# Portions of GDN's solve inside projections, and the residual's scale and bias behind y

## The chip, the cores and the metric

The kernel runs on one core of one Trainium2 chip. The metric is the device time of one execution in microseconds (us). Each version is run several times; the median counts.

## The reference, cut to what matters

A decoder trunk of four layers over 512 tokens of width 1024, in float32. Each layer has a token mixer (Gated DeltaNet, HGRN2, GLA, Gated DeltaNet) and a SwiGLU channel mixer; both add to the scaled residual and are followed by a layer norm.

```python
for i in range(DEPTH):
    m = mixer_i(x)                        # GDN, HGRN2, GLA, GDN
    x = layer_norm(DN_ALPHA * x + m, mix_ln_g[i], mix_ln_b[i])
    x = layer_norm(DN_ALPHA * x + swiglu(x, ffn_w_in[i], ffn_w_down[i]), ffn_ln_g[i], ffn_ln_b[i])

def gated_deltanet(...):                  # per chunk of 64 tokens
    L = strict_lower(einsum('bhncd,bhnsd->bhncs', k * beta, k) * decay)
    sol = triangular_solve(L + eye(CHUNK), [v * beta, k * beta * exp(G)])
    ...
    o = gated_rms_norm(o, z, norm_w)      # o * rsqrt(mean(o*o)) * norm_w * silu(z)
    return o @ w_out
```

## The kernel before

Tokens stand in NT = 4 row tiles of 128, the width in KD = 8 tiles of 128. A float32 product is made of three matmuls on TensorE (PE) of operands split in a high and a low part (`mm3`, lines 183, 184 and 185). Weights stream from DRAM on SyncE's queue; ScalarE (ACT) casts the high part (`whi`, L144) and VectorE (DVE) subtracts for the low part (`wlo`, L147). PSUM is two pools of four banks: `acc` holds projections (`pj`), `mx` the rest. A tile scheduler sets the order of each engine from the order in which the program is written and from its priorities; inside `manual_schedule` PE keeps the written order. `behind(ins)` holds operations on DVE behind the instruction `ins`.

**GDN's solve.** `gdn` takes the eight heads in two batches, in layers 0 and 3, so there are four solves. `values()` makes eight projections of a batch (v, v, z, z, v, v, z, z; each 24 matmuls of 128x512), and `solve` the inverse of the triangular matrices of 16 chunk blocks. It begins with a chain on DVE that ends in `td` and `ud` (two transposes, L849). Then come four stages of small matmuls on PE: the first (L859) and the second (L865) 64 of 16x16, the third (L877) and the fourth (L891) two bursts of 16 of 32x32 each; between two stages ACT or DVE copies the result (`yt`, `td`, `y2`). A trace counts two rows for one float32 matmul, so that 64 show as 128. Two stages of 64x64 (`y3`, L902 and L908) end the solve. `solve` is a generator: `yield 4` or `yield 1` lets as many projections be written ahead of what follows, and the first stage is held behind the last matmul of the fourth of them (`filled`).

**Output projection and norm.** `out_proj` reads the residual `x` (eight half tiles of 128x512, `get_x`) and calls `down_norm`. In layers 1, 2 and 3 what was stored is the normed residual without the scale and bias of the FFN norm, so `work` has to multiply each half tile by `lnp` (L256) and add `lnp` (L257): 16 operations on DVE. Four `lnp` tiles come by DMA into three buffers (tag `tr`). `work` is called once for each k in `down_part` and holds its operations behind `heads_end`, the last scaling `on*occ` of the heads (L533). The last heads are transposed on PE (`ytp`, L543), DVE makes `y` from them (L550), ACT its high part (`xTh`, L468), DVE its low part (`xTl`, L469); the matmuls `dn` of k = 6 and 7 (4 to 7 in layer 3) need these. `down_part` makes the first half of the columns for all row tiles, `add_x` (L352) adds them to x, `bn_stats` follows (L370). Of the second half, the program writes by hand the order on PE: `down(0)`, `down(1)`, three matmuls of `down(2)`, `tr(0)`, the rest of `down(2)`, and so on. `norm(i)` stands behind `down(i)`: `add_x`, `bn_stats`, the aggregate (L385) and nine small steps to L398 on DVE, then ACT norms the two halves of x (L403), and `tr(i)` transposes x on PE (`xtp`, L221).

Of the kernel before, what the change touches and what calls it, by code (L numbers as in the profile page):

```python
# [13 lines left out]
ALU = mybir.AluOpType  # L14
# [23 lines left out]
class Net:  # L38
    def __init__(self, ctx, tc, a, out):
        self.tc, self.nc, self.a, self.out = tc, tc.nc, a, out  # L40
        pool = lambda name, bufs, **kw: ctx.enter_context(tc.tile_pool(name=name, bufs=bufs, **kw))
        self.cp = pool("const", 1)
        self.raw = pool("raw", 2)
        self.wsp = pool("wsplit", 6)
        self.xp = pool("xT", 1)
        self.ar = pool("arena", 1)
        self.col = pool("cols", 2)
        self.mid = pool("mid", 1)
        self.dr = pool("dram", 2, space=bass.MemoryType.DRAM)
        self.acc = pool("acc", 4, space=PSUM)  # L50
        self.mx = pool("mx", 4, space=PSUM)
        self.n = 0
        self.deferred, self.late, self.lmask, self.x_gb = [], [], None, None
        self.norm_end = self.heads_end = None
        self.todo = []
        self.lo_eng = self.nc.vector
        self.xT = tuple(self.xp.tile([P, KD, T], F32R, name=n) for n in ("xTh", "xTl"))
        self.consts()
# [133 lines left out]
    def proj_cols(self, ps, wt, s, m=P):  # L192
        (wh, wl), (xh, xl) = wt, self.xT
        if wl is None:
            for k in range(KD):
                for x in (xl, xh):
                    self.nc.tensor.matmul(ps[:m, s], wh[:, k], x[:, k, s], start=k == 0 and x is xl,
                                          stop=k == KD - 1 and x is xh)
            return
        for k in range(KD):  # L200
            self.mm3(ps[:m, s], (wh[:, k], wl[:, k]), (xh[:, k, s], xl[:, k, s]), k == 0, k == KD - 1)

    def begin(self, wts):

# [134 lines left out]
    def down_part(self, kt, w, k0, dh, pool, alpha):  # L339

        ps = [self.bank(pool, [P, 512], "dn") for _ in range(NT)]
        k1 = k0 + len(kt)
        for k, wt in self.kblocks(w, dh, k0, k1):
            for i in range(NT):
                self.mm_tok(ps[i], i, kt[k - k0], wt, k == k0, k == k1 - 1)
            self.work()
        for i in range(NT):
            self.add_x(ps[i], i, dh, alpha)

# [5 lines left out]
    def down_norm(self, kt, w, k0, pools, alpha, g, b, to_dram, to_out, rtags):  # L355

        nc, V = self.nc, self.nc.vector
        n = len(kt)
# [156 lines left out]
    def finish(self, heads, ss, dv, nw, tag, facs=None):  # L515


        nc, V = self.nc, self.nc.vector
        n = len(heads)
        c = self.small([P, 2, n * NT], s="occ", bufs=2)  # L520
        if facs is not None:
            V.scalar_tensor_tensor(c[:, 0], ss, SCALE * SCALE / dv, facs[1], ALU.mult, ALU.mult)
            V.tensor_scalar(c[:, 0], c[:, 0], RMS_EPS, None, ALU.add)
        else:
            V.tensor_scalar(c[:, 0], ss, SCALE * SCALE / dv, RMS_EPS, ALU.mult, ALU.add)
        self.rsqrt(c[:, 1], c[:, 0], n * NT, "o")
        if facs is not None:
            V.scalar_tensor_tensor(c[:, 1], c[:, 1], SCALE, facs[0], ALU.mult, ALU.mult)
        else:
            V.tensor_scalar(c[:, 1], c[:, 1], SCALE, None, ALU.mult)  # L530
        todo = [(on, k, e) for k, (ons, gates) in enumerate(heads) for e, on in enumerate(ons)]
        for on, k, e in todo:
            op = V.tensor_tensor(on, on, c[:, 1, k * NT:(k + 1) * NT, None].broadcast_to([P, NT, P]), ALU.mult)  # L533
        self.heads_end = op.ins
        self.deferred += [(on, nw[e], heads[k][1][e], tag) for on, k, e in todo]

    def flush(self):

        todo, self.deferred = self.deferred, []
        for n, (on, nw, gate, tag) in enumerate(todo):  # L540
            pt = self.bank(self.mx, [P, T], "ytp")
            for i in range(NT):
                self.nc.tensor.transpose(pt[:, i * P:(i + 1) * P], on[:, i], self.ident)  # L543
            if tag == "yy":
                yy = yy if n % 2 else self.pair()
                y = yy[:, n % 2]
            else:
                y = self.t2(tag, s="y")
            gate = gate[0][gate[1]]
            self.nc.vector.scalar_tensor_tensor(y, pt, nw, gate, ALU.mult, ALU.mult)  # L550
            yield y

    def gdn(self, layer, j):
# [109 lines left out]
        for b in range(H // NB):  # L663
# [91 lines left out]
                        yield  # L755

            fill = values()
            for n in self.solve(ntf, gd):
                for _ in range(n):
                    next(fill, None)  # L760
            for _ in fill:
                pass

# [51 lines left out]
    def solve(self, nt, gd):  # L815
# [4 lines left out]
        hc = nt.shape[1]  # L820
# [26 lines left out]
        td, ud = sv((P, hc, 32), "td"), sv((P, hc, 32), "ud")  # L847
        for dst, src in ((td, U), (ud, U.rearrange("p s c -> p c s"))):
            V.transpose(dst.rearrange("p h (e c) -> p c e h", e=2), src[:, :, None, :].broadcast_to([P, 16, 2, 16]))  # L849
        yield 4  # L850
        filled = self.last_mm

        py = self.bank(self.mx, [P, 2, hc, 16], "iy")
        S.activation(py.rearrange("p a h c -> p (a h c)"), self.ident[:, None, :].broadcast_to([P, 4, P]), AF.Copy, scale=0.0)
        pu = py[:, 1]
        with self.behind(filled):
            for i in range(hc):
                for q, r in enumerate(half):
                    mm(py[r, 0, i], nt[r, i, 32 * q + 16:32 * q + 32], td[r, i, 0:16], start=True, stop=True)  # L859
        yt = sv((P, hc, 16), "yt")  # L860
        S.copy(yt, py[:, 0])
        yield 1
        for i in range(hc):
            for r in half:
                mm(pu[r, i], yt[r, i], ud[r, i, 16:32], start=True, stop=True)  # L865
        V.scalar_tensor_tensor(ud[:, :, 16:32], ud[:, :, 16:32], self.hi16[:, 1:2], pu, ALU.mult, ALU.add)
        V.tensor_scalar(ud[:, :, 0:16], ud[:, :, 0:16], self.hi16[:, 0:1], None, ALU.mult)
        V.transpose(td, ud)
        yield 1

        y2 = sv((P, hc, 32), "y2")
        pu = self.bank(self.mx, [P, hc, 32], "iu")
        py = self.bank(self.mx, [P, hc, 32], "iy")
        for q in (0, 2):
            r1, r2 = quads[q], quads[q + 1]
            for i in range(hc):
                mm(py[r2, i], nt[r1, i, r2], td[r1, i], start=True, stop=True)  # L877
            S.copy(y2[r2], py[r2])
        for r in quads:
            G.tensor_copy(nt[r, :, r], ud[r])  # L880
        hh = hc // 2
# [1 line left out]
        for g in range(2):  # L883
            G.memset(t64[g][0:32, :, 32:64], 0.0)
            for r in quads[:2]:
                S.copy(t64[g][r, :, r], td[r, g * hh:(g + 1) * hh])
        yield 1
        for q in (0, 2):
            r1, r2 = quads[q], quads[q + 1]
            for i in range(hc):  # L890
                mm(pu[r1, i], y2[r2, i], ud[r2, i], start=True, stop=True)  # L891
            if q == 0:
                for g in range(2):
                    V.transpose(t64[g][32:64, :, 0:32], pu[r1, g * hh:(g + 1) * hh])
            V.tensor_copy(nt[r1, :, r2], pu[r1])
        yield 1
        lo, up = slice(0, 64), slice(64, P)
        for g in range(2):
            y3 = sv((P, hh, 64), "y3")
# [1 line left out]
            for i in range(hh):  # L901
                mm(py[up, i], nt[lo, g * hh + i, up], t64[g][:, i], start=True, stop=True)  # L902
            S.copy(y3[up], py[up])
            if g == 0:
                yield 1
            pw = self.bank(self.mx, [P, hh, 64], "iw")
            for i in range(hh):
                mm(pw[lo, i], y3[up, i], nt[up, g * hh + i, up], start=True, stop=True)  # L908
# [322 lines left out]
```

## Time and profile before

| | |
|---|---|
| runs, median | 2725.11, 2723.51, 2724.34; 2724.34 us |
| the profiled execution | 2725.05 us, its span 2723.3 us |
| PE busy | 2664.1 us, 98% |
| DVE busy | 1520.1 us, 56% |
| ACT busy | 1060.2 us, 39% |
| DMA | 251.43 MB, 92 GB/s |
| mean granted clock of PE | 0.993 |

The span is the time from the first to the last instruction that the profiler saw; the profiled execution is one run, timed like the others. A granted clock of 1.00 is PE at 2.4 GHz, 0.50 at 1.2 GHz.

### The profile page before, as it was taken

The numbers are of one execution on the slowest core, as the hardware profiler recorded it, in microseconds if no ns is written. First come the engines' busy times: TensorE is split into PE (matmuls) and PEld (weight loads), VectorE is DVE, ScalarE is ACT, GpSimd is POOL, SyncE is SP. The second block draws the span as 40 slices with busy tenths as digits, with TensorE's granted clock in tenths as the row PEclk, the third lists the DMA queues.
The fourth block names the chain that finished last, engine by engine and source line by source line (L and its number), as shares of the span: only waits on it lengthen the run. The fifth ranks groups of instructions, "written<-read, shape, count | busy, mean of one in ns | idle before, by whom it ended". The sixth has DMA issues, their size and how long they took to land.

```text
span 2723.3 us, 37712 instructions
## 1 busy us (share of the span) xinstructions
PE 2664.1 (98%) x15279; PEld 2224.7 (82%) x15279; DVE 1520.1 (56%) x3155; ACT 1060.2 (39%) x2123; POOL 90.3 (3%) x176
## 2 busy tenths in 40 slices
PE   9999999999999999999999999999999999999998
PEld 8787888888877778888887878888887887888886
DVE  7676653333777786323366676323378586833235
ACT  5464442122544434222254634222255554422220
POOL 1000000001000000000000000000010100000000
PEclk9999999999999999999999999999999999999999
DMA  5213223223221332223321332232322132322321
GB/s 158 63 48 101 86 94 108 93 93 109 93 78 47 97 120 93 93 98 103 110 95 63 96 122 93 93 104 97 109 94 78 48 101 78 101 93 93 99 87 62
DMA packets 199678, 251.43 MB, mean 92 GB/s; under 512 B 9082, under 2 KB 152576, under 8 KB 199504
## 3 DMA queue, kind: packets, MB, share of 16 engines
q1 hardware_dynamic: 195152, 237.29, 27.1%
q0 software_dynamic: 4352, 11.73, 1.5%
q8 instruction: 120, 1.97, 0.3%
q14 instruction: 54, 0.44, 0.1%
HBM read 240.61 MB, written 8.39 MB: 91 GB/s over the span
## 4 chain that ended last, share of the span: by engine, by line
PE 81%; DVE 12%; ACT 4%; issue 2%; DMA 1%; POOL 0%; SPq 0%; DVEq 0%; ACTq 0%; POOLq 0%
PE pj L183 16%; PE pj L184 16%; PE pj L185 16%; PE dn L183 7%; PE dn L184 7%; PE dn L185 7%; DVE am L932 2%; DVE wlo L147 1%; ACT junk L702 1%; PE sc L965 1%; PE kk L689 1%; DVE qk L631 1%; PE xtp L221 1%; PE vp L183 1%; PE vp L184 1%
## 5 line engine op out<-in xcount | busy, mean ns | idle before, releaser
L183 PE MATMUL pj<-xTl,whi 128*128 128x512 f32 (+1 forms) x2472 | 925.9, 375 | 0.0
L184 PE MATMUL pj<-xTh,whi 128*128 128x512 f32 (+1 forms) x2472 | 922.3, 373 | 0.0
L185 PE MATMUL pj<-xTh,wlo 128*128 128x512 f32 (+1 forms) x2472 | 922.1, 373 | 0.0
L144 ACT CAST whi<-wraw 128x1024 fp32r<-128x1024 f32 x400 | 420.1, 1051 | 1179.4 <-PE pj L184 796.1
L147 DVE TENSOR_TENSOR wlo<-wraw,whi 128x1024 fp32r<-128x1024 f32 x400 | 487.9, 1222 | 633.5 <-ACT whi L144 633.2
L183 PEld LDWEIGHTS pj<-xTl,whi 128*128 128x128 f32 x2472 | 468.6, 190 | 78.0 <-issue 0.7
L185 PEld LDWEIGHTS pj<-xTh,wlo 128*128 128x128 f32 x2472 | 468.2, 189 | 77.7 <-issue 0.5
L184 PEld LDWEIGHTS pj<-xTh,whi 128*128 128x128 f32 x2472 | 468.5, 190 | 77.0 <-issue 0.7
L453 DVE TENSOR_TENSOR sg<-sg,pj 128x512 f32<-128x512 f32 x88 | 60.5, 687 | 247.4 <-PE pj L185 247.0
L183 PE MATMUL dn<-wlo,hhi 128*128 128x512 f32 x416 | 161.8, 389 | 0.0
L184 PE MATMUL dn<-whi,hhi 128*128 128x512 f32 x416 | 161.8, 389 | 0.0
L185 PE MATMUL dn<-whi,hlo 128*128 128x512 f32 x416 | 161.8, 389 | 0.0
L352 DVE SCALAR_TENSOR_TENSOR x<-x,dn 128x512 f32<-128x512 f32 x96 | 64.5, 684 | 69.1 <-PE dn L185 69.1
L185 PEld LDWEIGHTS dn<-whi,hlo 128*128 128x128 f32 x416 | 78.1, 188 | 16.3
L183 PEld LDWEIGHTS dn<-wlo,hhi 128*128 128x128 f32 x416 | 78.1, 188 | 16.2
L184 PEld LDWEIGHTS dn<-whi,hhi 128*128 128x128 f32 x416 | 78.1, 188 | 16.2
L183 PE MATMUL dn<-wlo,nt 128*128 128x512 f32 x224 | 87.5, 390 | 0.0
L184 PE MATMUL dn<-whi,nt 128*128 128x512 f32 x224 | 87.1, 389 | 0.0
L185 PE MATMUL dn<-whi,nt 128*128 128x512 f32 x224 | 87.1, 389 | 0.0
L183 PE MATMUL dn<-wlo,xTh 128*128 128x512 f32 x192 | 77.5, 404 | 2.8 <-ACT xTh L468 2.8
L184 PE MATMUL dn<-whi,xTh 128*128 128x512 f32 x192 | 75.9, 395 | 0.0
L185 PE MATMUL dn<-whi,xTl 128*128 128x512 f32 x192 | 74.9, 396 | 0.0
(388 smaller groups left out, 3310.7 us busy)
## 6 DMA issues: line engine op xcount, KB each, us to landing
wraw<-in_ffn_w_in SPq DMA_DIRECT2D x88, 1024.0 KB, 5.1
wraw<-in_ffn_w_down SPq DMA_DIRECT2D x40, 1024.0 KB, 5.0
wraw<-in_gdn_w_in SPq DMA_DIRECT2D x32, 1024.0 KB, 5.8
wraw<-in_hgrn_w_in SPq DMA_DIRECT2D x16, 1024.0 KB, 5.8
wraw<-in_gla_w_in SPq DMA_DIRECT2D x12, 1024.0 KB, 5.2
wraw<-in_gdn_w_out SPq DMA_DIRECT2D x8, 1024.0 KB, 5.1
xd<-x SPq DMA_DIRECT2D x24, 256.0 KB, 2.0
x<-xd SPq DMA_DIRECT2D x24, 256.0 KB, 6.5
```

The costliest lines, as they stand in the source:

```text
L144: nc.scalar.copy(hi, raw)
L147: (eng or nc.vector).tensor_tensor(lo, raw, hi.bitcast(F32), ALU.subtract)
L183: mm(out, ah, bl, start=start, stop=False)
L184: mm(out, ah, bh, start=False, stop=False)
L185: self.last_mm = mm(out, al, bh, start=False, stop=stop).ins
L221: nc.tensor.transpose(ps[:, k], src[:, k * P:(k + 1) * P], self.ident)
L352: self.nc.vector.scalar_tensor_tensor(s, s, alpha, ps, ALU.mult, ALU.add)
L453: nc.vector.tensor_tensor(s, s, pss[2 + j], ALU.mult)
L631: V.scalar_tensor_tensor(dst[:, T - n:], ps[:, :n], wc(t), dst[:, T - n:], ALU.mult, ALU.add)
L689: mm(pk[:, i], k[:, sl], src[:, sl], start=True, stop=True)
L702: S.activation(junk, ptk[:, i], AF.Square, accum_out=ss[:, n_src, lh * NT + i:lh * NT + i + 1])
L932: V.copy_predicated(av[:, c, js], self.lmask[b][:, gs], pm[:, c, gs])
```

## The change

Three things change. (1) `solve` no longer writes the small matmuls of a stage as one burst: each of the four stages is cut into four portions (16 matmuls of 16x16, or 8 of 32x32), and `proj_cols` writes one portion behind k = 1, 3, 4 and 5 of a projection, with PE's order as written. `filled` is gone. (2) `down_part` calls `work` only at the last two k, for two half tiles each, and `down_norm` lets the other four follow behind `down_part`. (3) `heads_end` is the last `y` made so far, no longer the last `on*occ`.

```diff
@@ -52,7 +52,7 @@
-        self.todo = []
+        self.todo, self.side = [], []
@@ -199,6 +199,8 @@
         for k in range(KD):
             self.mm3(ps[:m, s], (wh[:, k], wl[:, k]), (xh[:, k, s], xl[:, k, s]), k == 0, k == KD - 1)
+            if self.side and k in (1, 3, 4, 5):
+                self.side.pop(0)()
@@ -343,7 +345,8 @@
                 self.mm_tok(ps[i], i, kt[k - k0], wt, k == k0, k == k1 - 1)
-            self.work()
+            if k >= k1 - 2:
+                self.work(2)
         for i in range(NT):
             self.add_x(ps[i], i, dh, alpha)
@@ -366,6 +369,7 @@
         self.down_part(kt, w, k0, 0, pools[0], alpha)
+        self.work(NT)
         for i in range(NT):
             V.bn_stats(stats[:, i, 0], self.x[i][0])
@@ -530,8 +534,7 @@
         for on, k, e in todo:
-            op = V.tensor_tensor(on, on, c[:, 1, k * NT:(k + 1) * NT, None].broadcast_to([P, NT, P]), ALU.mult)
-        self.heads_end = op.ins
+            V.tensor_tensor(on, on, c[:, 1, k * NT:(k + 1) * NT, None].broadcast_to([P, NT, P]), ALU.mult)
@@ -547,7 +550,7 @@
-            self.nc.vector.scalar_tensor_tensor(y, pt, nw, gate, ALU.mult, ALU.mult)
+            self.heads_end = self.nc.vector.scalar_tensor_tensor(y, pt, nw, gate, ALU.mult, ALU.mult).ins
             yield y
@@ -755,9 +758,13 @@
             fill = values()
-            for n in self.solve(ntf, gd):
-                for _ in range(n):
-                    next(fill, None)
+            for n, side in self.solve(ntf, gd):
+                self.side = side
+                with self.tc.manual_schedule(engines={mybir.EngineType.PE}) if side else nullcontext():
+                    for _ in range(n):
+                        next(fill, None)
+                    while self.side:
+                        self.side.pop(0)()
@@ -847,35 +854,47 @@
-        yield 4
-        filled = self.last_mm
+        yield 4, None
+
+        def parts(f, n, step):
+
+            def run(i0):
+                for i in range(i0, i0 + step):
+                    f(i)
+            return [lambda i0=i0: run(i0) for i0 in range(0, n, step)]
...
-        with self.behind(filled):
-            for i in range(hc):
-                for q, r in enumerate(half):
-                    mm(py[r, 0, i], nt[r, i, 32 * q + 16:32 * q + 32], td[r, i, 0:16], start=True, stop=True)
+
+        def first(i):
+            for q, r in enumerate(half):
+                mm(py[r, 0, i], nt[r, i, 32 * q + 16:32 * q + 32], td[r, i, 0:16], start=True, stop=True)
+
+        yield 1, parts(first, hc, 4)
         yt = sv((P, hc, 16), "yt")
         S.copy(yt, py[:, 0])
-        yield 1
...
+        yield 1, parts(second, hc, 4)
...
+        yield 1, parts(third, 2 * hc, 8)
...
+        yield 1, parts(fourth, 2 * hc, 8)
@@ -901,8 +922,6 @@
             S.copy(y3[up], py[up])
-            if g == 0:
-                yield 1
```

The line numbers grow by up to 15: L859 becomes L872, L865 L880, L550 L553, L469 L473, L256 and L257 become L258 and L259, L352 L355, L385 L389.

On PE, in the second solve of layer 0 (`iy` is the PSUM tile of the first two stages), before: the first stage follows one matmul behind the fifth projection, and four matmuls part it from the second.

```order
L185 MATMUL pj_452_2627<-xTh_84,wlo_432_2444 128x512
L183 MATMUL pj_454_2725<-xTl_85,whi_437_2484 128x512
L859 MATMUL iy_448_2555<-td_416_2385,nt_213_1521 16x16 x64
L184 MATMUL pj_454_2725<-xTh_84,whi_437_2484 128x512
L185 MATMUL pj_454_2725<-xTh_84,wlo_438_2486 128x512
L183 MATMUL pj_454_2725<-xTl_85,whi_437_2484 128x512
L184 MATMUL pj_454_2725<-xTh_84,whi_437_2484 128x512
L865 MATMUL iy_448_2555<-ud_417_2386,yt_449_2621 16x16 x64
L185 MATMUL pj_454_2725<-xTh_84,wlo_438_2486 128x512
L183 MATMUL pj_454_2725<-xTl_85,whi_437_2484 128x512
```

After, the same place:

```order
L183 MATMUL pj_467_2869<-xTl_85,whi_449_2571 128x512
L184 MATMUL pj_467_2869<-xTh_84,whi_449_2571 128x512
L185 MATMUL pj_467_2869<-xTh_84,wlo_450_2573 128x512
L872 MATMUL iy_448_2567<-td_416_2397,nt_213_1533 16x16 x16
L183 MATMUL pj_451_2575<-xTl_85,whi_431_2454 128x512
L184 MATMUL pj_451_2575<-xTh_84,whi_431_2454 128x512
L185 MATMUL pj_451_2575<-xTh_84,wlo_432_2456 128x512
L183 MATMUL pj_451_2575<-xTl_85,whi_431_2454 128x512
L184 MATMUL pj_451_2575<-xTh_84,whi_431_2454 128x512
L185 MATMUL pj_451_2575<-xTh_84,wlo_432_2456 128x512
L872 MATMUL iy_448_2567<-td_416_2397,nt_213_1533 16x16 x16
L183 MATMUL pj_451_2575<-xTl_85,whi_431_2454 128x512
```

The scheduler draws the first six matmuls of each of the projections 5 to 8 (`pj_451`, `pj_454`, `pj_461`, `pj_467`) ahead of the first portion, 24 in all; then portions and six, three, three and six matmuls of a projection take turns.

On DVE, in the output projection of layer 1 (HGRN2), before, the last of the 16 operations with `lnp`, then the two `y` of the last heads:

```order
L257 TENSOR_TENSOR x_1373_8772<-x_1373_8772,lnp_1379_8788 128x512
L256 TENSOR_TENSOR x_1375_8774<-x_1375_8774,lnp_1378_8787 128x512
L147 TENSOR_TENSOR wlo_1423_9014<-wraw_1421_9010,whi_1422_9012 128x1024
L550 SCALAR_TENSOR_TENSOR y_1403_8932<-ytp_1402_8927,cw_917_5862,zg_1340_8653 128x512
L550 SCALAR_TENSOR_TENSOR y_1405_8955<-ytp_1404_8950,cw_917_5862,zg_1344_8685 128x512
L257 TENSOR_TENSOR x_1375_8774<-x_1375_8774,lnp_1379_8788 128x512
L469 TENSOR_TENSOR xTl_85<-y_1403_8932,xTh_84 128x512
L469 TENSOR_TENSOR xTl_85<-y_1405_8955,xTh_84 128x512
L147 TENSOR_TENSOR wlo_1425_9018<-wraw_1421_9010,whi_1424_9016 128x1024
L147 TENSOR_TENSOR wlo_1428_9024<-wraw_1426_9020,whi_1427_9022 128x1024
L352 SCALAR_TENSOR_TENSOR x_1368_8767<-x_1368_8767,dn_1388_8807 128x512
L352 SCALAR_TENSOR_TENSOR x_1370_8769<-x_1370_8769,dn_1389_8808 128x512
```

After, the same place, from `wlo` to the second low part:

```order
L147 TENSOR_TENSOR wlo_1425_9042<-wraw_1421_9034,whi_1424_9040 128x1024
L553 SCALAR_TENSOR_TENSOR y_1403_8944<-ytp_1402_8939,cw_917_5886,zg_1340_8677 128x512
L258 TENSOR_TENSOR x_1368_8791<-x_1368_8791,lnp_1376_8803 128x512
L258 TENSOR_TENSOR x_1370_8793<-x_1370_8793,lnp_1376_8803 128x512
L473 TENSOR_TENSOR xTl_85<-y_1403_8944,xTh_84 128x512
L259 TENSOR_TENSOR x_1368_8791<-x_1368_8791,lnp_1377_8804 128x512
L259 TENSOR_TENSOR x_1370_8793<-x_1370_8793,lnp_1377_8804 128x512
L553 SCALAR_TENSOR_TENSOR y_1405_8969<-ytp_1404_8964,cw_917_5886,zg_1344_8709 128x512
L258 TENSOR_TENSOR x_1372_8795<-x_1372_8795,lnp_1376_8803 128x512
L258 TENSOR_TENSOR x_1374_8797<-x_1374_8797,lnp_1376_8803 128x512
L473 TENSOR_TENSOR xTl_85<-y_1405_8969,xTh_84 128x512
L259 TENSOR_TENSOR x_1372_8795<-x_1372_8795,lnp_1377_8804 128x512
```

Half of the 16 operations now stand between and behind the two `y`, ahead of `add_x`; the other eight follow behind the four `add_x` of the first half of the columns and ahead of their `bn_stats`.

On DVE, later in the same output projection, before, `norm(0)` (`lnc_1431`) alone, with `add_x` of row tile 1 (`dn_1407`) behind its last step L398 (some steps are left out):

```order
L370 BN_STATS bnst_1387_8806<-x_1374_8773 128x6
L147 TENSOR_TENSOR wlo_1430_9028<-wraw_1426_9020,whi_1429_9026 128x1024
L352 SCALAR_TENSOR_TENSOR x_1369_8768<-x_1369_8768,dn_1406_8981 128x512
L382 BN_STATS bnst_1387_8806<-x_1369_8768 128x6
L385 BN_AGGR lnc_1431_9058<-bnst_1387_8806 128x2
L386 TENSOR_SCALAR lnc_1431_9058<-lnc_1431_9058 128x1
L390 SCALAR_TENSOR_TENSOR lnc_1431_9058<-lnc_1431_9058 128x1
L398 SCALAR_TENSOR_TENSOR lnc_1431_9058<-lnc_1431_9058 128x1
L352 SCALAR_TENSOR_TENSOR x_1371_8770<-x_1371_8770,dn_1407_8982 128x512
L382 BN_STATS bnst_1387_8806<-x_1371_8770 128x6
```

After:

```order
L147 TENSOR_TENSOR wlo_1428_9048<-wraw_1426_9044,whi_1427_9046 128x1024
L147 TENSOR_TENSOR wlo_1430_9052<-wraw_1426_9044,whi_1429_9050 128x1024
L355 SCALAR_TENSOR_TENSOR x_1369_8792<-x_1369_8792,dn_1406_9005 128x512
L355 SCALAR_TENSOR_TENSOR x_1371_8794<-x_1371_8794,dn_1407_9006 128x512
L386 BN_STATS bnst_1387_8830<-x_1369_8792 128x6
L386 BN_STATS bnst_1387_8830<-x_1371_8794 128x6
L389 BN_AGGR lnc_1431_9082<-bnst_1387_8830 128x2
L389 BN_AGGR lnc_1432_9121<-bnst_1387_8830 128x2
L390 TENSOR_SCALAR lnc_1431_9082<-lnc_1431_9082 128x1
L390 TENSOR_SCALAR lnc_1432_9121<-lnc_1432_9121 128x1
L391 TENSOR_SCALAR lnc_1431_9082<-lnc_1431_9082 128x1
L391 TENSOR_SCALAR lnc_1432_9121<-lnc_1432_9121 128x1
```

`add_x` of row tile 1 now stands ahead of the chain of row tile 0, and the two chains take turns step by step.

## Rows read from the trace of the kernel before

**Rows 1.** The waits view of PE: what it waited for, us in total, times, longest us.
```profile
PE iy L859 <- DVE td L849: 6.3, 4, 1.8
...
PE dn L183 <- DVE yy L550: 4.8, 1, 4.8
...
PE iy L865 <- issue: 4.3, 4, 1.4
...
PE dn L183 <- ACT xTh L468: 2.8, 2, 1.6
...
PE xtp L221 <- ACT x L403: 1.6, 4, 0.4
```

**Rows 2.** Timeline of PE in the first solve: start, us, operation, idle before.
```profile
108.24 1.21 PE L859 MATMUL iy<-td,nt 16*16 16x16 f32 x128 [1.76 <-DVE td L849]
109.38 0.50 PE L183 MATMUL pj<-xTl,whi 128*128 128x512 f32 x1
109.72 0.40 PE L184 MATMUL pj<-xTh,whi 128*128 128x512 f32 x1
109.95 0.39 PE L185 MATMUL pj<-xTh,wlo 128*128 128x512 f32 x1
110.27 0.37 PE L865 MATMUL iy<-ud,yt 16*16 16x16 f32 x28
112.09 1.01 PE L865 MATMUL iy<-ud,yt 16*16 16x16 f32 x100 [1.45 <-issue]
```

**Rows 3.** Stretches behind solves 1, 3 and 4, then 2 us of solve 4; busy us (instructions) by engine, PEclk.
```profile
113.03:118.32 5.29, 5.29 (x20) 4.13 (x13) 1.19 (x2) 0.41 (x1) 2.98 (x6) 0.50 0.03 6
...
2110.87:2114.88 4.01, 4.01 (x18) 3.14 (x10) 1.19 (x2) 0.42 (x1) 2.98 (x6) 0.50 0.01 4
...
2249.78:2255.06 5.28, 5.28 (x20) 4.13 (x13) 2.27 (x4) 0.63 (x1) 3.37 (x7) 0.50 0.01 3
...
2247.00:2249.00 2.00, 1.97 (x124) 1.44 (x123) 2.00 (x4) 0.81 (x2) 0.00 (x0) 0.87 0.03 8
```

**Rows 4.** Timeline of PE, output projection of layer 1: ytp and tr(0).
```profile
999.89 1.03 PE L543 MATMUL ytp<-ident,on 128*128 128x128 f32 x8
...
1019.28 1.04 PE L221 MATMUL xtp<-ident,x 128*128 128x128 f32 x8
```

**Rows 5.** Timeline of DVE in the same stretch.
```profile
990.69 1.29 DVE L256 TENSOR_TENSOR x<-x,lnp 128x512 f32<-128x512 f32 x2
...
1002.06 1.40 DVE L550 SCALAR_TENSOR_TENSOR y<-ytp,cw,zg 128x512 f32<-128x512 f32 x2
...
1005.18 2.35 DVE L147 TENSOR_TENSOR wlo<-wraw,whi 128x1024 fp32r<-128x1024 f32 x2
...
1007.45 2.52 DVE L352 SCALAR_TENSOR_TENSOR x<-x,dn 128x512 f32<-128x512 f32 x4
...
1009.88 2.46 DVE L370 BATCH_NORM_STATS2 bnst<-x 128x6 f32<-128x512 f32 x4
...
1014.84 0.21 DVE L385 BATCH_NORM_AGGREGATE lnc<-bnst 128x2 f32<-128x12 f32 x1
...
1016.80 0.16 DVE L398 SCALAR_TENSOR_TENSOR lnc<-lnc 128x1 f32<-128x1 f32 x1
```

**Rows 6.** Timeline of ACT in the same stretch.
```profile
1017.00 1.52 ACT L403 ACTIVATE x<-x,lnc 128x512 f32<-128x512 f32 x2 [6.66 <-DVE lnc L398]
```

**Rows 7.** Timelines of DVE and PE, output projection of layer 3.
```profile
2307.66 1.29 DVE L256 TENSOR_TENSOR x<-x,lnp 128x512 f32<-128x512 f32 x2
...
2313.28 0.75 PE L183 MATMUL dn<-nt,xTh 128*128 128x512 f32 x1 [4.82 <-DVE yy L550]
...
2337.62 1.03 PE L221 MATMUL xtp<-ident,x 128*128 128x128 f32 x8
```

**Rows 8.** Windows behind PE's waits of layers 3 and 2; columns as in rows 3.
```profile
2313.00:2317.00 4.00, 3.72 (x9) 2.63 (x10) 3.79 (x7) 1.24 (x2) 1.08 (x2) 0.57 0.55 152
...
1616.00:1618.00 2.00, 2.00 (x11) 1.61 (x10) 1.33 (x3) 0.00 (x0) 0.00 (x0) 1.00 1.06 368
```

More of the change, by code (lines that the diff above doesn't have):

```diff
@@ L855, in solve, with second @@
         pu = py[:, 1]
-        with self.behind(filled):
-            for i in range(hc):
-                for q, r in enumerate(half):
-                    mm(py[r, 0, i], nt[r, i, 32 * q + 16:32 * q + 32], td[r, i, 0:16], start=True, stop=True)
+        def first(i):
+            for q, r in enumerate(half):
+                mm(py[r, 0, i], nt[r, i, 32 * q + 16:32 * q + 32], td[r, i, 0:16], start=True, stop=True)
+        yield 1, parts(first, hc, 4)
         yt = sv((P, hc, 16), "yt")
         S.copy(yt, py[:, 0])
-        yield 1
-        for i in range(hc):
+        def second(i):
             for r in half:
                 mm(pu[r, i], yt[r, i], ud[r, i, 16:32], start=True, stop=True)
+        yield 1, parts(second, hc, 4)
         V.scalar_tensor_tensor(ud[:, :, 16:32], ud[:, :, 16:32], self.hi16[:, 1:2], pu, ALU.mult, ALU.add)
@@ L873, in solve, with third @@
         py = self.bank(self.mx, [P, hc, 32], "iy")
-        for q in (0, 2):
+        def third(i):
+            q, i = i // hc * 2, i % hc
             r1, r2 = quads[q], quads[q + 1]
-            for i in range(hc):
-                mm(py[r2, i], nt[r1, i, r2], td[r1, i], start=True, stop=True)
-            S.copy(y2[r2], py[r2])
+            mm(py[r2, i], nt[r1, i, r2], td[r1, i], start=True, stop=True)
+            if i == hc - 1:
+                S.copy(y2[r2], py[r2])
+        yield 1, parts(third, 2 * hc, 8)
         for r in quads:
@@ L886, in solve, with fourth @@
                 S.copy(t64[g][r, :, r], td[r, g * hh:(g + 1) * hh])
-        yield 1
-        for q in (0, 2):
+        def fourth(i):
+            q, i = i // hc * 2, i % hc
             r1, r2 = quads[q], quads[q + 1]
[L890 to L896, printed above, removed]
+            mm(pu[r1, i], y2[r2, i], ud[r2, i], start=True, stop=True)
+            if i == hc - 1:
+                if q == 0:
+                    for g in range(2):
+                        V.transpose(t64[g][32:64, :, 0:32], pu[r1, g * hh:(g + 1) * hh])
+                V.tensor_copy(nt[r1, :, r2], pu[r1])
+        yield 1, parts(fourth, 2 * hc, 8)
         lo, up = slice(0, 64), slice(64, P)
@@ L903, in solve @@
             S.copy(y3[up], py[up])
-            if g == 0:
-                yield 1
             pw = self.bank(self.mx, [P, hh, 64], "iw")
```

## The prediction

> **What bounds the kernel.** TensorE (PE) is busy for 98% of the span, so the time can only change where PE stands still, runs at its lower clock, or gets more to do. I therefore read the waits of PE first [rows 1], then the two places that the change touches: GDN's solve (there are four: two batches of heads in layers 0 and 3), and the stretch from the last heads' transposes (ytp) to the first transposes of the normed residual (xtp, tr(0)) in the output projections of layers 1, 2 and 3. Layer 0 has no scale and bias to apply.
>
> In a solve the reader is to see three losses [rows 2]. PE waits 1.76 us for td, which comes from VectorE (DVE); there are four such waits, 6.3 us together [rows 1]. The second burst of small matmuls breaks off after 28 rows and goes on 1.45 us later, with only "issue" as releaser; four such gaps take 4.3 us [rows 1]. And after it the granted clock is 0.50, the 1.2 GHz level, for 5.29, 5.28, 4.01 and 5.28 us [rows 3]. In 19.9 us of that, half the time is 9.9 us; by the 49 weight loads counted there at the 0.23 us of a matmul at the 2.4 GHz level (109.72 to 109.95, [rows 2]) 8.6 us is lost. I take 9.2 us for the four.
>
> In the output projections PE waits because the first y on DVE stands behind the residual's scale and bias: 4.8 us in layer 3, and 2.8 us in layers 1 and 2, 1.2 and 1.6 [rows 1]. In layer 1 DVE gives 989.5 to 1002 almost wholly to those operations, and y comes at 1002.06 [rows 5]. From ytp at 999.89 to tr(0) at 1019.28 PE takes 19.4 us, 1.2 of it that wait [rows 4]; before tr(0) it does not wait.
>
> **The solves, part by part.** The number of small matmuls stays. *td:* the first portion follows 24 full matmuls of projections 5 to 8 as the first burst followed 24 before, or one fewer, 0.23 us, in two solves: the wait stays, 6.3 + 0.45 us. *The issue gaps:* bounds are 4.3 us kept and all of it gone. The gap came 28 rows into the second of two long bursts; a portion has 32 rows or 16 and 0.7 to 1.4 us of full matmuls (3 to 6 of 0.23) behind it. I take it as gone: -4.3. *The clock:* a 1.6 us wait followed by full matmuls leaves the granted clock at 1.00 [rows 8], and that is now the pattern: the td wait, then portions of 0.3 us between full matmuls. Bounds are 0 and -9.2; I take -9.2. *The seams:* behind a burst the second matmul starts 0.34 us after the first (109.38 to 109.72), and ahead of the next burst 0.32 us pass (109.95 to 110.27), where 0.23 is usual [rows 2]. One burst thus costs 0.11 + 0.09 = 0.2 us beyond its own work. Bursts per solve go from 1 + 1 + 2 + 2 = 6 to 4 x 4 = 16, so 10 more in each of four solves: +8.0 us; bounds 0 (no row has a portion) and 8. What DVE and ScalarE (ACT) do for the next stage lies beside 6 full matmuls, 1.4 us, and that cover is only slightly over what a copy needs. Sum: +0.45 - 4.3 - 9.2 + 8.0 = -5.0 us.
>
> A rule of the Trainium skill speaks against this part. "TensorE: Matmul & The Clock Gate", section "A second HAM failure mode: psum-queue depth-cycling", tells of a kernel in which frequent very short idles of TensorE between groups of matmuls made the clock swing between its two levels. By it the sixteen seams would keep the loss of 9.2 us, and the solves would come to +4.2 instead of -5.0.
>
> **The output projections.** The waits for the first y go, and the residual's work comes to stand behind it. What is queued behind that matters: add_x, bn_stats, and the chain of small steps that ends in tr(0). Two things are late. First, DVE now has all of this between ytp and tr(0), in layer 1: 0.5 for the first four transposes; 2 y 1.4; 2 xTl and 16 x operations at 0.60 each (two of that form in 1.29 with 0.09 of overlap) 1.2 + 9.6; 4 add_x 2.5; 4 bn_stats 2.4; 2 wlo 2.3; 2 add_x 1.3; 2 bn_stats 1.3; the aggregate and its nine steps 2.3 (2.1 for one row tile, 1014.84 to 1016.96, now two row tiles in turn); [rows 5] then ACT's first half, 0.76 of 1.52, and 0.15 to start [rows 6]. That is 25.7 us, so tr(0) starts at 1025.6. PE itself would be there at 1019.28 - 1.21 = 1018.1: it stalls 7.5 us, and against before tr(0) is 6.3 us later. Second, even if DVE were in time, the order has add_x of row tile 1 ahead of the chain of row tile 0, and that needs PE's matmuls of row tile 1, which end only 0.7 us before tr(0): 0.65 + 1.3 + 2.3 + 0.9 = 5.2 us behind them, so a stall of 4.5 us is the floor.
>
> The second four transposes of tr(0) then wait for ACT's second half: 0.76 less the 0.45 of the first four, +0.3. tr(1) finds its row tile ready: its wait of 0.4 [rows 1] and its own 0.3 go, -0.7. Behind such a stall the clock drops: after the 4.8 us of layer 3 it was 0.57 on average over 4 us, nine matmuls in 3.72 us instead of 2.1 [rows 8], 1.6 us lost; with 7.5 us of idle I take the same, bounds 0 and the 2.5 of a solve. So layer 1 has +6.3 + 0.3 - 0.7 + 1.6 = +7.5. Layer 2 has the same order and a wait of 1.6 that goes: +7.1. In layer 3 the chain starts at 2307.66 with four y, four xTl and three wlo: 2.65 + 2.4 + 9.6 + 2.5 + 2.4 + 3.4 + 1.3 + 1.3 + 2.3 + 0.9 = 28.8 us, and about 1.2 in which the first add_x waits for PE: tr(0) at 2337.6, where it is now [rows 7]. The gain at 2313 (wait and low clock) is all given back in a stall of 5.7 us there (PE would be ready at 2337.62 - 1.6 - 4.1 = 2331.9); with the same small terms +0.3 - 0.7 + 1.6 layer 3 has +1.2. Sum: +15.8 us. The wlo that move ahead of y wait for nothing (ACT is free), the DMAs keep their order.
>
> **Total.** The profiled execution took 2725.05 us (span 2723.3), 0.7 above the median of 2724.34. 2725.05 + 15.8 - 5.0 = 2735.8; as a median **2735.1 us**, 0.4% slower. About 0.2%, 5.4 us, is what a measurement of this kernel can tell from no change: 2718.9 to 2729.8 counts as the same.
>
> **Rivals.**
> *The clock still falls in the solve.* For it: in the last solve the clock begins to fall (0.87) in two microseconds in which PE is busy for 1.97, nearly all of it with small matmuls [rows 3], so these seem to count for little. Against: full matmuls now take most of every stretch there. +9.2: 2744; with the issue gaps kept too 2749. The Trainium skill's rule above would lead to this case. Chance 0.2.
> *Cheap portions, or the stall at its floor.* Seams that cost nothing make 2735.1 - 8.0 = 2727; stalls of 4.5 instead of 7.5, 7.5 and 5.7 make 2735.1 - 7.2 = 2728. Both together 2720. The first is open, since no row has a portion; the second needs 3 of DVE's 25.7 us to lie beside something else, and its queue has no gap in which they could. Chance 0.2, of it 0.04 for under 2718.9.
> *Faster: DVE ends before PE wants tr(0).* Then only the waits go: -1.2 - 1.6 - 4.8 - 1.6 (clock) - 5.0 = -14.2, 2710. It decides when DVE's work from ytp to tr(0) takes under 18.2 us (19.4 - 1.2) in layers 1 and 2. DVE has 25.7 us there, and the printed order sets a floor of its own; only a trace in which the operations run in another order than printed would do it. Chance 0.06.
> *The change doesn't do what it says.* The work stands behind the first y, not the last, and the first portion still waits for td; both are in the sum.
>
> **How the numbers follow.** The forecast has 0.54: its bounds (seams 6 to 8, stalls +-2 each, clock 0 to 2.5 each) give 2728 to 2742. The rivals have 0.2, 0.2 and 0.06. The range of 2722 to 2747 leaves out the faster rival (0.06), the cheap case with both parts (0.04) and the clock's rival with the gaps kept (0.08). Faster by over 0.2%: 0.06 + 0.04 = 0.10. The same: 0.16 of the cheap case and 0.03 of the forecast's edge, 0.19. Slower: 0.71.
>
> **What would show it.** In the profile after: waits of PE for ACT's x (L403 before, at tr(0)) of 5 to 8 us at three places with granted clock under 1.00 behind them; no wait for y or xTh; the td waits as before; no issue gap; a granted clock of 1.00 through all four solves; 0.3 us on both sides of each portion. Waits at tr(0) under 2 us would make the forecast wrong at its largest term; granted clocks of 0.50 in the solves would make it wrong upward.

## The result, and the profile after

The changed kernel takes 2741.27 us (median of four runs, 2736.52 to 2743.37) against 2724.73 us of before in the same comparison: a ratio of 1.0059, 95% interval 1.0043 to 1.0074. It is slower by 16.5 us. The forecast was 2735.1 us, its range 2722 to 2747.

The profiled execution took 2742.6 us with a span of 2740.9, 17.6 us more than before's. Part 1 of its page has TensorE (PE) busy for 10 us more, although its instructions are the same in number (before, then after):

```profile
PE 2664.1 (98%) x15279; PEld 2224.7 (82%) x15279; DVE 1520.1 (56%) x3155; ACT 1060.2 (39%) x2123; POOL 90.3 (3%) x176
...
PE 2674.1 (98%) x15279; PEld 2221.8 (81%) x15279; DVE 1519.5 (55%) x3155; ACT 1058.8 (39%) x2123; POOL 94.3 (3%) x176
```

The waits view of PE (what it waited for, us in total, times, longest) answers to [rows 1]:

```profile
PE xtp L223 <- ACT x L407: 19.5, 4, 7.0
...
PE iy L872 <- DVE td L856: 6.3, 4, 1.7
...
PE ytp L546 <- DVE on L537: 2.0, 2, 1.0
```

The waits for the first y (4.8 and 2.8 us) and the four issue gaps (4.3 us) are gone. In their place PE waits 19.5 us for ScalarE's (ACT) normed x, 19.1 us of it in three waits ahead of tr(0); the td waits are what they were. New are two waits of 1.0 us for the scaling of the last heads in layers 0 and 3.

Where the 17.6 us lie is read from the same transposes in both timelines. Each row is a stretch of the program between two of them; the last column is how much longer it is now.

| stretch | before, us | after, us | longer by |
|---|---|---|---|
| start to tr(0) of layer 0's output projection, solves 1 and 2 | 0 to 334.13 | 0 to 336.19 | 2.1 |
| layer 1, ytp of its first heads to tr(3) | 973.41 to 1038.79 | 975.49 to 1046.85 | 6.0 |
| layer 2, last ytp to tr(3) | 1611.29 to 1650.58 | 1619.28 to 1665.09 | 6.5 |
| layer 3, up to the last ytp, solves 3 and 4 | 2014.04 to 2306.21 | 2028.40 to 2323.66 | 3.1 |
| layer 3, last ytp to tr(3) | 2306.21 to 2357.12 | 2323.66 to 2374.81 | 0.2 |

So the output projections cost 12.7 us and the solves with what surrounds them 5.2 us; everywhere else the two timelines run side by side, to 0.3 us.

**The output projections.** In PE's timeline, ytp of layer 1 and tr(0) of layers 1, 2 and 3 (start, us, operation, idle before it) answer to [rows 4, 7]:

```profile
1000.73 1.03 PE L546 MATMUL ytp<-ident,on 128*128 128x128 f32 x8
...
1025.99 1.97 PE L223 MATMUL xtp<-ident,x 128*128 128x128 f32 x8 [6.96 <-ACT x L407]
...
1644.55 1.97 PE L223 MATMUL xtp<-ident,x 128*128 128x128 f32 x8 [6.96 <-ACT x L407]
...
2354.05 1.97 PE L223 MATMUL xtp<-ident,x 128*128 128x128 f32 x8 [5.19 <-ACT x L407]
```

VectorE (DVE) works through the whole stretch in layer 1 without a pause, as its timeline shows (against [rows 5]):

```profile
1001.37 0.75 DVE L553 SCALAR_TENSOR_TENSOR y<-ytp,cw,zg 128x512 f32<-128x512 f32 x1 [3.57 <-PE ytp L546]
...
1008.71 2.47 DVE L355 SCALAR_TENSOR_TENSOR x<-x,dn 128x512 f32<-128x512 f32 x4
...
1011.10 1.29 DVE L258 TENSOR_TENSOR x<-x,lnp 128x512 f32<-128x512 f32 x2
...
1015.92 2.46 DVE L374 BATCH_NORM_STATS2 bnst<-x 128x6 f32<-128x512 f32 x4
...
1018.30 2.34 DVE L147 TENSOR_TENSOR wlo<-wraw,whi 128x1024 fp32r<-128x1024 f32 x2
...
1020.56 1.27 DVE L355 SCALAR_TENSOR_TENSOR x<-x,dn 128x512 f32<-128x512 f32 x2
...
1024.93 0.28 DVE L402 SCALAR_TENSOR_TENSOR lnc<-lnc 128x1 f32<-128x1 f32 x2
```

From y at 1001.37 the residual's work, add_x, the second eight operations, bn_stats, two wlo, then both add_x of row tiles 0 and 1 follow one another; L402 ends the two chains at 1025.2, and tr(0) starts at 1025.99. From ytp to tr(0) that is 25.3 us. Behind the stall PE runs at 1.2 GHz, half its clock (windows; busy us and instructions by engine, then PEclk):

```profile
1026.00:1028.00 2.00, 2.00 (x9) 2.00 (x10) 0.77 (x2) 2.00 (x4) 0.00 (x0) 0.50 0.00 0
1028.00:1030.00 2.00, 2.00 (x6) 1.52 (x6) 2.00 (x5) 1.54 (x5) 0.00 (x0) 0.50 0.00 0
```

**The solves.** The first portion of the first solve and the second one, in PE's timeline (against [rows 2]):

```profile
108.61 0.38 PE L872 MATMUL iy<-td,nt 16*16 16x16 f32 x32 [1.66 <-DVE td L856]
...
108.92 0.50 PE L183 MATMUL pj<-xTl,whi 128*128 128x512 f32 x1
...
109.26 0.39 PE L184 MATMUL pj<-xTh,whi 128*128 128x512 f32 x1
...
110.52 0.38 PE L872 MATMUL iy<-td,nt 16*16 16x16 f32 x32
...
110.83 0.50 PE L183 MATMUL pj<-xTl,whi 128*128 128x512 f32 x1
```

The wait for td stands as before; a portion of 32 rows takes 0.31 us to the next full matmul. Behind a portion the second full matmul again starts 0.34 us after the first. The windows over the four solves, from the td wait on (PEclk is the third number from the end):

```profile
108.00:121.00 13.00, 12.39 (x293) 8.55 (x294) 6.39 (x9) 2.74 (x5) 0.70 (x2) 1.00 0.17 58
246.50:258.00 11.50, 10.87 (x203) 7.07 (x206) 5.14 (x8) 3.15 (x5) 0.00 (x0) 0.70 0.08 28
2120.50:2132.00 11.50, 11.21 (x217) 7.50 (x218) 2.94 (x5) 2.01 (x3) 0.00 (x0) 0.70 0.15 52
2262.00:2275.00 13.00, 12.73 (x296) 8.84 (x296) 8.28 (x13) 4.22 (x7) 1.05 (x2) 1.00 0.04 15
```

In solves 1 and 4 the granted clock stays at 1.00; in 2 and 3 it falls. Yet solves 1 and 3 have the same matmuls in the same order on PE, and so have 2 and 4. The four runs took 2736.5 to 2743.4 us at mean granted clocks of 0.995 to 0.992, the slower the lower the clock.

### The profile page after: what moved, and what is told of

The parts are those of the page before. It is cut to its first block, busy times and chain, and to the rows that moved or that the text cites. A ratio compares the mean times of both kernels' runs of the same rounds, so it can differ in the third digit from the quotient of the medians.

```text
span 2740.9 us, 37708 instructions
## 1 busy us (share of the span) xinstructions
PE 2674.1 (98%) x15279; PEld 2221.8 (81%) x15279; DVE 1519.5 (55%) x3155; ACT 1058.8 (39%) x2123; POOL 94.3 (3%) x176
## 4 chain that ended last, share of the span: by engine, by line
PE 81%; DVE 13%; ACT 4%; issue 1%; DMA 1%; SPq 0%; DVEq 0%; ACTq 0%
PE pj L183 16%; PE pj L184 16%; PE pj L185 16%; PE dn L183 7%; PE dn L184 7%; PE dn L185 7%; DVE wlo L147 2%; DVE am L951 1%; PE sc L984 1%; ACT junk L705 1%; PE xtp L223 1%; PE kk L692 1%; DVE qk L634 1%; PE vp L183 1%; PE vp L184 1%
## 5 line engine op out<-in xcount | busy, mean ns | idle before, releaser
L355 DVE SCALAR_TENSOR_TENSOR x<-x,dn 128x512 f32<-128x512 f32 x96 | 64.3, 684 | 65.4 <-PE dn L185 65.4
```

The source lines that it names most:

```text
L355: self.nc.vector.scalar_tensor_tensor(s, s, alpha, ps, ALU.mult, ALU.add)
```

## The experiments

All times are medians of several rounds beside runs of the kernel before on the same chip: 2724.49 us for e1 to e4, 2724.28 for e5 to e8, 2725.63 for e9 and e10.

**e1: the portions alone.** The change, with `work`, its calls and `heads_end` as before.

```diff
-            if k >= k1 - 2:
-                self.work(2)
+            self.work()
...
-        self.work(NT)
...
+        self.heads_end = op.ins
```

> Only the portions of the solve; the residual's scale and bias stand as before. Theory: a portion costs about 0.24 us beyond its own work and cutting a burst another 0.05, ten more a solve, +12 us over four solves; the four issue gaps go, -4.3; the clock falls in some solves and not in others, 2.6 us each, so -9.7 plus 0 to 4 times 2.6. With two falls as in the profile of the change +4 to +5: median about 2729, runs spread over 2723 to 2734. Rival: the two halves of the change hang together (the portions push work of VectorE into the output projections), and alone the portions cost nothing or gain: 2715 to 2724.

Measured: 2727.66 us (2724.59 to 2731.75), ratio 1.0010 (1.0001 to 1.0019). The portions alone gain nothing. In the profiled execution (2725.97 us, mean granted clock 0.997) the clock fell in one solve, the second, and for a short while: 0.86 over 247 to 259 us, 1.00 over the same stretch of the other three. The runs above 2727.7 us have means of 0.996 and 0.995, those below 0.997, but for one of 0.995 (2727.2 us). The rival (alone they gain) falls.

**e2: the residual's work alone.** Before, with the second and third part of the change.

```diff
-            self.work()
+            if k >= k1 - 2:
+                self.work(2)
...
+        self.work(NT)
...
-        self.heads_end = op.ins
...
+            self.heads_end = self.nc.vector.scalar_tensor_tensor(y, pt, nw, gate, ALU.mult, ALU.mult).ins
```

> Only the residual's work behind the last y; the solve as before. Theory: stalls of 7.0, 7.0 and 5.2 us ahead of tr(0) in layers 1, 2 and 3 with low clock behind them, against waits of 1.2, 1.6 and 4.8 us that go: +12 to +13, 2737, with a narrow spread of the runs. Rival: part of the 12.6 us there comes from the solve's portions, and alone this half costs under 8 us: below 2733.

Measured: 2739.21 us (2736.14 to 2739.37), ratio 1.0049 (1.0037 to 1.0062): +14.7 us, above the +12 to +13 expected. Its waits view has the same 19.5 us, and the issue gaps of the uncut solve:

```profile
PE xtp L221 <- ACT x L405: 19.5, 4, 7.0
...
PE iy L866 <- issue: 4.8, 4, 1.3
```

With e1's 3.2 us the sum is 17.9, against 16.5 for both together: the two halves add up.

**e3: no hold.** Before, with the residual's operations held behind nothing.

```diff
-            with self.behind(self.heads_end):
+            with nullcontext():
                 V.tensor_tensor(x, x, g, ALU.mult)
```

> Before, with the residual's 16 operations held behind nothing: the scheduler puts them ahead of the last heads' scaling, where VectorE has idle time. Theory (VectorE's work between the first y and tr(0) is what stalls TensorE): the waits for y of 1.2, 1.6 and 4.8 us and the low clock behind the last go and no stall comes: 2715 to 2718. Rival: an operation that waits for its residual or lnp tile holds up the heads' small steps behind it on VectorE, and TensorE waits there: 2724 or more, with new waits of the small matmuls for VectorE ahead of the output projections.

Measured: 2719.19 us (2715.42 to 2722.22), ratio 0.9979 (0.9970 to 0.9988): 5.3 us faster than before, and 1.2 us above the range expected. PE's timeline, layer 1 and then layer 3:

```profile
998.96 1.03 PE L543 MATMUL ytp<-ident,on 128*128 128x128 f32 x8
...
1005.04 0.50 PE L183 MATMUL dn<-wlo,xTh 128*128 128x512 f32 x1 [0.92 <-ACT xTh L468]
...
1019.21 1.04 PE L221 MATMUL xtp<-ident,x 128*128 128x128 f32 x8
...
2305.12 2.46 PE L543 MATMUL ytp<-ident,on 128*128 128x128 f32 x16 [1.11 <-DVE on L533]
...
2330.21 1.03 PE L221 MATMUL xtp<-ident,x 128*128 128x128 f32 x8
```

In layer 3 no matmul waits for yy, and from ytp to tr(0) PE takes 25.1 us instead of 31.4; that is most of the gain. In layer 1 the operations run from 981.2 to 992.9, taking turns with the small steps of the heads' scaling, which ends 5.3 us later (996.0 instead of 990.7) and still ahead of ytp; waits of 0.9 and 0.6 us for xTh and xTl remain. The rival's price is there, though small: these operations wait three times for their residual, 3.6 us in the three layers together, and twice for `lnp`, 1.6 us; and ytp of layer 3 now waits 1.1 us for the last scaling of the heads, where before it did not. Whether these operations cause that wait is not shown.

**e4: eight and eight.** Before, with eight operations behind the last scaling of the heads and eight behind the last y.

```diff
-            self.work()
+            if isinstance(kt, Lazy):
+                if k < k0 + 4:
+                    self.work()
+                if k == k1 - 1:
+                    self.work(NT, self.y_end)
+            else:
+                self.work()
```

> Before, with eight of the 16 operations behind the last scaling of the heads as before and eight behind the last y. Theory: in layers 1 and 2 the first y is on time and VectorE has 4.8 us less behind it than in the change, so the stall of 7.0 shrinks to about 2 or none (the order has row tile 0's chain ahead of row tile 1's add): -1 to -3 us there; in layer 3 the first y still waits behind eight operations, 4.8 us, and has eight behind it: 0 to -2. Together 2720 to 2724. Rival: the stall is not set by the amount of VectorE's work but by the order of the two chains, then layers 1 and 2 lose nothing and gain the full waits of 2.8 us even with the work behind y; or it stays near 7 us there and the time is above 2730.

Measured: 2728.29 us (2726.86 to 2730.94), ratio 1.0014 (1.0005 to 1.0023): a miss, slower than before.

```profile
PE xtp L221 <- ACT x L409: 6.1, 4, 2.6
...
PE dn L183 <- DVE yy L556: 4.8, 1, 4.8
```

The stall shrinks from 7.0 to 2.6 us in layers 1 and 2, as the amount of work says, but the expectation forgot to set that 2.6 against the waits of 1.2 and 1.6 us that go, and left out the low clock behind the stall (0.79 over 1016 to 1024 us). In layer 3 y still waits 4.8 us. e4 differs from the change in the order of the chains too: row tile 0's `bn_stats` and first steps stand ahead of row tile 1's `add_x`; what that order is worth is seen in e8.

**e5: two portions a stage.** e1 with eight portions in a solve instead of sixteen.

```diff
-            if self.side and k in (1, 3, 4, 5):
+            if self.side and k in (1, 4):
...
-        yield 1, parts(first, hc, 4)
+        yield 1, parts(first, hc, 8)
```

> The solve's portions alone as in e1, but two a stage (behind k = 1 and 4) instead of four, 8 in a solve. Theory: 8 portions fewer a solve at 0.24 + 0.05 us are 9 us less than e1's 2727.7, if the clock falls as seldom and the issue gaps stay away: 2718 to 2721. Rival: longer bursts bring the falls back in all four solves (2.6 us each) and a burst of 64 rows may break off again: 2724 to 2729, no better than e1.

Measured: 2716.60 us (2714.62 to 2719.27), ratio 0.9970 (0.9958 to 0.9981): 11.1 us less than e1, a little more than expected. The waits for td are all there, the issue gaps stay away, and the clock still falls in some solves, in this execution towards the end of the first (139 to 147) and at the start of the third. The first of these falls comes some 30 us behind the td wait:

```profile
PE iy L871 <- DVE td L855: 6.3, 4, 1.7
```
```profile
108.00:121.00 13.00, 12.80 (x322) 10.11 (x323) 6.59 (x11) 4.05 (x6) 1.94 (x4) 1.00 0.15 49
...
139.00:147.00 8.00, 8.00 (x40) 6.05 (x39) 4.82 (x18) 3.48 (x6) 3.68 (x6) 0.79 0.49 134
...
2098.00:2111.00 13.00, 11.34 (x242) 8.19 (x244) 5.79 (x8) 2.01 (x3) 0.00 (x0) 0.87 0.28 83
```

**e6: td covered.** e5 with five projections ahead of the first stage.

```diff
-        yield 4, None
+        yield 5, None
```

> As e5, with five instead of four projections written ahead of the first stage, so that 30 full matmuls instead of 24 stand ahead of the first portion; the fourth stage loses its projection as cover. Theory: the td waits of 1.6 us shrink to about 0.3, -5 us, and without that idle the clock does not fall in any solve; the fourth stage pays some 1 us a solve where nothing covers it: e5 less 3 to 8 us, runs within 3 us of each other. Rival: the small matmuls themselves, not the td wait, let the clock fall: half-clock stretches stay in the trace and only the td waits go.

Measured: 2712.76 us (2711.18 to 2714.04), ratio 0.9954 (0.9940 to 0.9967): 3.8 us less than e5, with runs within 2.9 us.

```profile
PE iy L871 <- DVE td L855: 1.5, 4, 0.4
```
```profile
109.00:122.00 13.00, 12.55 (x300) 9.65 (x299) 10.08 (x14) 3.58 (x6) 0.37 (x1) 1.00 0.39 116
244.00:257.00 13.00, 12.30 (x298) 9.14 (x298) 10.56 (x15) 4.83 (x8) 0.00 (x0) 1.00 0.22 75
2098.50:2111.00 12.50, 12.05 (x297) 9.37 (x297) 9.58 (x14) 3.45 (x6) 0.00 (x0) 1.00 0.37 105
2233.50:2246.00 12.50, 11.84 (x296) 8.86 (x295) 10.02 (x15) 4.67 (x8) 0.57 (x1) 1.00 0.24 70
```

The td waits are 0.4 us each, and the granted clock is 1.00 over all four solves, with the same eight portions. The rival (the small matmuls alone let the clock fall) does not hold here. The edit also moves the portions apart: 9, 15, 9, 15, 9, 9 and 11 full matmuls stand between them, where e5 has 9, 9, 9, 9, 9, 11 and 9 or 10.

**e7: both.** e6 with e3's edit.

> e6 and e3 together: two portions a stage, five projections ahead, and the residual's 16 operations held behind nothing. Theory (the two halves of the program do not touch each other): e6 less the 5.3 us of e3. Rival: the residual's operations now meet the solves' chain or the moved projections on VectorE in layers 0 and 3, and less than half of the 5.3 us comes.

Measured: 2705.56 us (2704.13 to 2707.75), ratio 0.9929 (0.9917 to 0.9942). It is 7.2 us less than e6, somewhat more than e3's 5.3, and 18.7 us faster than before: the best of all. What PE still waits for at the two places:

```profile
PE iy L871 <- DVE td L855: 1.5, 4, 0.4
...
PE ytp L545 <- DVE on L535: 1.8, 2, 1.1
...
PE dn L185 <- DVE xTl L471: 0.6, 1, 0.6
...
PE dn L183 <- ACT xTh L470: 0.5, 1, 0.5
```

The td waits are 0.4 us each, the wait for yy is gone, and no full matmul of this execution's solves ran at half clock. The last ytp of layers 0 and 3 waits 1.8 us for the scaling of the heads, 0.4 more than in e6. The rival does not hold: the two edits add up.

**e8: one chain first.** e2, with add_x of a row tile held behind the norm chain of the row tile before.

```diff
-            V.bn_stats(stats[:, i, 1], self.add_x(ps[i], i, 1, alpha))
+            with self.behind(self.chain_end if i and not to_out else None):
+                x1 = self.add_x(ps[i], i, 1, alpha)
+            V.bn_stats(stats[:, i, 1], x1)
```

> e2 (the residual's work behind the last y, the solve as before) with add_x of a row tile held behind the norm chain of the row tile before it, so that row tile 0's chain is not paired with row tile 1's. Theory (the amount of VectorE's work between the first y and tr(0) sets the stall): tr(0) comes only about 1.3 us earlier at three places, one add_x and one bn_stats, and tr(1) pays up to 0.7 of it back: 2736 to 2739, against 2739.2 of e2. Rival: the order of the two chains sets the stall; then it shrinks from 7 to 2 us or less and the time falls to 2724 to 2728.

Measured: 2736.63 us (2735.49 to 2737.54), ratio 1.0043 (1.0030 to 1.0055), 2.6 us less than e2. Layer 1 of its timeline:

```profile
999.81 1.03 PE L546 MATMUL ytp<-ident,on 128*128 128x128 f32 x8
...
1024.11 1.97 PE L221 MATMUL xtp<-ident,x 128*128 128x128 f32 x8 [6.03 <-ACT x L407]
```

The stall is 6.0 us where it was 7.0. The order of the chains is worth one add_x and one bn_stats; the amount of work ahead of them sets the rest.

**e9: whole bursts, further apart.** Before, with `yield 5` instead of `yield 4`: the first stage stands where it stood, and 23 or 24 full matmuls part the first three stages.

> Before, with five instead of four projections written ahead of the first stage and nothing cut: the first stage stands where it stood, behind 25 full matmuls, so the td wait stays, but 23 or 24 full matmuls now part it from the second stage and that from the third, where 3 to 5 and 18 stood. Theory (it is the td wait, the two bursts and the issue gap close together that let the clock fall, and the gap comes of two bursts close together): gaps and falls go, -4.3 and up to -9.9, with 6 bursts a solve as before and some 1 us a solve where the fourth stage has less cover: 2711 to 2717. Rival: a whole burst of 64 small matmuls behind the td wait is enough for the clock to fall: falls in most solves, 2719 to 2724.

Measured: 2718.98 us (2717.40 to 2721.13), ratio 0.9977 (0.9968 to 0.9987): between the theory's range and the rival's.

```profile
PE iy L859 <- DVE td L849: 4.9, 3, 1.8
...
PE iy L877 <- ACT y L878: 0.3, 1, 0.3
```
```profile
108.00:121.00 13.00, 12.64 (x297) 10.60 (x298) 8.76 (x13) 2.69 (x5) 0.96 (x2) 0.87 0.23 63
2101.00:2114.00 13.00, 12.50 (x296) 10.47 (x297) 8.62 (x13) 2.80 (x5) 0.69 (x2) 0.87 0.21 60
```

No wait for issue is left; the td waits stay (three, and a fourth of 1.4 us that is put down to ACT's vf), and a small one of 0.3 us ahead of the third stage is new. In this execution the clock falls behind the td wait in solves 1 and 3, where 0.87 on average over 13 us is 3.4 us at half clock, and holds in the other two. So two bursts and a gap close together are not needed for a fall, but without them it is shorter and rarer than before, where all four solves fall and the first has 0.74 over the same 13 us, 6.8 us at half clock.

**e10: e9 with e3's edit.**

> e9 with the residual's 16 operations held behind nothing, as e3 had them. Theory: e9 less 5 to 7 us, beside e7's 2705.6. Rival: the operations now delay the chain that td waits for, and less than half of it comes.

Measured: 2710.87 us (2707.72 to 2713.88), ratio 0.9944 (0.9932 to 0.9957): 8.1 us less than e9, so the rival does not hold, but 5.3 more than e7 beside which it was expected. In its profiled execution the td waits stand as in e9, the clock falls in solves 1 and 4, and it falls once more in layer 1's output projection, behind waits of 0.9, 0.9 and 0.6 us for xTh and xTl (0.72 over 1002 to 1008 us). The runs spread over 6 us, e7's over 3.6.

## Why the prediction was right, and where its sum was wrong

**The direction and the mechanism of the output projections were right.** The 25.7 us that were added up for DVE from ytp to tr(0) measured 25.3, and the stalls of 7.5, 7.5 and 5.7 us measured 6.96, 6.96 and 5.19. The new place of the work turns 4.8 + 2.8 us of waits into 19.1 us of stalls, without an instruction more. e2 shows this half alone at +14.7 us, against +15.8 forecast. e4 and e8 tell the amount of work from the order of the chains: half the work behind y, in the other order, leaves 2.6 us of stall, and the other order by itself takes away 1.0. The forecast was somewhat high for layer 2 (+7.1, measured 6.5) and for layer 3 (+1.2, measured 0.2: from ytp to tr(0) PE takes 30.4 us, where the sum had the 31.4 of before). For layer 1 it was near (+7.5): the 6.0 of the table hold a gain of 1.2 us ahead of the last ytp, which e6 and e9 have there too, with the output projections of before, so that the change does not make it; from the last ytp to tr(3) PE takes 38.9 us before and 46.1 after, +7.2. The low clock behind the stall was there, 0.50 from 1026 to 1030.

**The sum of the solves was wrong: -5.0 forecast, +5.2 measured.** That the time still lies near the forecast is in part luck: the solves came out 10.2 us above it, the output projections 3.1 below. Two terms of the solves' sum were off.

*The clock, -9.2.* It was taken as regained in all four solves. In the profiled execution it fell again in two: there the full matmuls between the first and the last small burst took 6.3 us more than 0.227 each, in the other two 3.8, so 2.5 us a fall and 5.0 us back. The step that failed is "a 1.6 us wait followed by full matmuls leaves the granted clock at 1.00, and that is now the pattern". The row read for it had full matmuls alone behind the wait; in the solve every third to sixth is followed by a portion. The rival "the clock still falls in the solve" came halfway true, and not the same in each run. e6 and e7 point to the td wait: with it covered none of their eight solves falls, where nine of twenty fall in the change, e1, e5, e9 and e10, in the profiled executions. That the wait alone is the cause is not shown: one of e5's two falls comes long behind it, and e6 also has more full matmuls between some portions. Against the spacing speaks e9, which has 23 or 24 between its first three bursts and falls in two solves with the wait in place. Whole bursts with the wait covered were not run. That the portions' short pauses alone would do it, as the section "A second HAM failure mode: psum-queue depth-cycling" of "TensorE: Matmul & The Clock Gate" in the Trainium skill tells of another kernel, the runs do not bear out: solves 1 and 4 of the change have sixteen portions and a granted clock of 1.00, e6 has eight and 1.00 everywhere. Why the same order falls in one solve and not in the other stays open.

*The seams, +8.0.* A portion costs more than the 0.2 us that was read. Between the first and last small burst of solve 1, 82 full matmuls took 22.39 us in the change, 3.78 more than 0.227 each, with sixteen portions, and 79 took 19.97 in e5, 2.04 more, with eight: 0.22 us a portion. The rest of the stretch, small matmuls and eight transposes, took 12.46 and 11.97: another 0.06. Forty portions more at 0.28 are 11.2 us. The Trainium skill's "TensorEngine Tiling (Array Packing)", section "Key Properties", says that a change of the tiling mode drains TensorE; 0.22 us at each portion agrees with that, though no run here separates a drain from anything else.

With these the solves come to -4.3 (issue gaps, as forecast) - 9.9 + 5.0 (clock; 9.9 is the prediction's upper count of the loss) + 11.2 = +2.0. Read without these prices, what the four solves take from their first to their last small burst beyond 0.227 us for each full matmul, the transposes left out, grows from 63.8 to 65.3 us, +1.5. Two more parts of the 5.2 us are seen. PE waits 1.0 us at the last ytp of layers 0 and 3 for the heads' scaling, 2.0 us together: right ahead of it stand 20 dn matmuls instead of 26, as some are drawn ahead into solves 2 and 4 (14 instead of 10 between the first and last small burst), and they no longer cover it. And 0.5 us come in the first 17 us of the program, ahead of any change. Some 0.7 to 1.2 us are not assigned.

*The other points.* No wait for y or xTh, td waits as before, no issue gap: as forecast. "A granted clock of 1.00 through all four solves": wrong in two. The faster rival (DVE ends before tr(0)) asked for under 18.2 us of DVE's work there; it had 25.3. That a hold elsewhere reaches that side is what e3 shows: the same 16 operations ahead of the heads' scaling cost nothing that comes near the waits they end.

## What to carry to other kernels

Work that is moved off one wait lands on the next: add up what the engine then has to do up to the next point where the bottleneck waits for it, and compare with the bottleneck's own time over that stretch (25.3 against 18.2 us here). Idle time ahead of the critical chain is the place for such work: the same 16 operations took 5 us off the kernel there and put 15 us on it behind the chain. Before a burst is cut into portions to keep the clock up, cover the wait ahead of it; each cut has a price (0.28 us here), and two portions a stage with the wait covered (e6, -11.5 us) beat two without (e5, -7.7 us) and four without (e1, +3.2 us). Much of that comes without any cut: whole bursts moved further apart (e9) give -6.7 us.

## What was not expected of the hardware

The granted clock is not a function of the instruction order alone: the same order fell in solve 2 and held in 4, fell in 3 and held in 1, and runs of the same program spread over 7 us (2736.5 to 2743.4) with their mean granted clock. e6, without the td waits, spread over 2.9 us; but e2, whose clock falls in all four solves, spread over 3.2, so that a narrow spread alone does not tell that the clock holds. The break in the second burst of small matmuls (1.45 us after 28 rows) came back neither in any of the portions nor in whole bursts of 64 with 24 full matmuls between them (e9); what causes it was not tried further.
